# First pair of each part of the down projection by seven products, a reordered plain pair ahead of it, and operand forms fetched in place

## The chip, the cores and the metric

The kernel runs on one core of one Trainium2 chip. The metric is device time in microseconds (us) of one execution; lower is better. TensorE is called PE below, VectorE DVE, ScalarE ACT, GpSimd POOL and SyncE SP, as the profile's page calls them.

## The reference: what is computed

One decoder layer over 512 prompt tokens and 8 sample tokens (520 columns in all, `NTOK`), width 2048, feed-forward width 5632, all in fp32. The part that matters here is the end of the layer:

```python
xn2 = rmsnorm(h, norm_ffn)
gu = xn2 @ w_gate_up
h = h + (jax.nn.silu(gu[..., :D_FF]) * gu[..., D_FF:]) @ w_down
y = rmsnorm(h, norm_final)
```

The last product, `@ w_down`, is the down projection. It follows the gate and up projections and ends just ahead of the final norm and the stores.

## The kernel before

**Precision.** Every fp32 operand is cut into a high part, which ACT rounds (`act.copy` to fp32r), and a low part, which DVE subtracts. A product of 128 by 128 weights with 260 columns (`HALF`) takes three matmuls for each 128 rows of the inner dimension: high by high, high by low, low by high. These are lines 1225 to 1227, in `passes`.

**Tiling.** Work goes by pairs of output tiles of 128 rows (`Pair`), with the inner dimension halved and the columns halved: a 2 by 2 by 2 block product, A11 to A22 for weights and B11 to B22 for activations. Activations in the two cut parts are called forms (`forms[name]` is a high and a low tile). A plain pair takes eight block products. A pair in Strassen's scheme (Winograd's variant) takes seven, M1 to M7, with weights S1 to S4 (sums of A blocks, `add`, line 1247) and forms T1 to T4 (differences of B blocks, computed once). `FORM` names what each product multiplies; `STEADY` gives the order M1, M4, M7, M6, M5, M2, M3.

**Parts.** The down projection splits its inner dimension into three parts (`SIZES` = 7, 7 and 8 steps of 128 for each half), since not all forms fit into SBUF. Each part goes through all eight pairs of output tiles, in the order `ORDER`, and adds to the residual in `mix` (line 1818 adds one operand, line 1819 the second). Forms of a part come from `a_d` in DRAM, where POOL wrote them during the gate and up projections (`to_dram`, lines 1410 to 1413, after `gated`, line 1404).

**A change of parts, before.** `cross` takes two plain pairs: the last of the old part and the first of the new one. Forms are replaced one by one, as soon as the old part has read them for the last time. The scheme between is `run`, over the six pairs left (seven in the last part). `fetch` (line 1776) brings a form from `a_d` into staging tiles `st` (spare rows of `mix` in the first part), two steps to a DMA of POOL's queue; `fill` lets ACT cast the staging into the high tile (line 1785) and DVE write the low one (line 1786). The tables `TAIL`, `LAST` and `HEAD` say after which product of a pair which loads (`+`), cuts, sums and fills are issued.

**Order and buffers.** From the out projection on, instructions stand on each engine in the order of the code. In `strassen`, step i issues the sum of weights for product i + 4, the cut of weights for product i + 3 (ACT line 1218, DVE line 1219), the product i, and then what combines it (`combine`, lines 1270 to 1275, and `out`). Cut weights go round four pairs of buffers (three of `wpl`, one of an extra pool), so a cut waits until PE has read the buffer four cuts back. Products accumulate in eight PSUM banks, five of them called `dn` and taken in turn. Weights come through SP's queue, one block of A to a DMA, into three `raw` buffers and one for A21.

Of the kernel before, what the change touches and what calls it, by code (L numbers as in the profile page):

```python
# [69 lines left out]
def decoder_kernel(ctx, tc, x_prompt, x_sample, state_delta, state_conv, state_pool, norm_mix, w_in,  # L70
# [1158 lines left out]
    class Pair:  # L1229
# [51 lines left out]
        def plain(self, hook):  # L1281

            w = self.w
            a, (b0, *c) = [pst()[:, :HALF] for _ in range(2)], [pst()[:, :HALF] for _ in range(3)]
            passes(a[0], w["A11"], "B11")
            passes(a[1], w["A21"], "B11")
            hook(0)
            for i in range(2):
                act.copy(cm[:, i, :], a[i])
            passes(b0, w["A12"], "B21")  # L1290
            passes(c[0], w["A11"], "T1", stop=False)
            self.cut("A22")
            hook(1)
            self.out(0, 0, cm[:, 0, :], b0)
            passes(c[1], w["A21"], "T1", stop=False)
            hook(2)
            passes(c[0], w["A12"], "B22", start=False)
            b1 = pst()[:, :HALF]
            passes(b1, w["A22"], "B21")
            hook(3)  # L1300
            self.out(0, 1, cm[:, 0, :], c[0])
            self.out(1, 0, cm[:, 1, :], b1)
            passes(c[1], w["A22"], "B22", start=False)
            hook(4)
            self.out(1, 1, cm[:, 1, :], c[1])
# [51 lines left out]
    def strassen(pairs, r21, hook, extra, order=FIRST):  # L1357
# [8 lines left out]
        for i, (q, n) in enumerate(steps):  # L1366
            j = i % 7
            hook(q, j)
            if q + 1 < len(pairs):
                swap = q + 2 == len(pairs) and order is FIRST  # L1370
                name = {0: "A21", 2: "A11", 3: "A12" if swap else "A22", 4: "A22" if swap else "A12"}.get(j)
                if name:
                    pairs[q + 1].load(name, r21 if name == "A21" else None)
            (p, name), (p4, name4) = block(i + 3), block(i + 4)
            pool_ = extra if i % 4 == 0 else wpl
# [3 lines left out]
            if name and (name != "S4" or lastly):  # L1379
                p.cut(name, pool_)  # L1380
# [4 lines left out]
            if name == "S4" and not lastly:  # L1385
                p.cut(name, pool_)
# [186 lines left out]
    strassen(ops, r21o, between, sc0, STEADY)  # L1573
# [187 lines left out]
    stage, spare, staged = [], [], {}  # L1761

    def fetch(name, part_):

        n = SIZES[part_]
        staged[name] = []
        for r in range(0, n, 2):
            k = min(2, n - r)
            if part_ == 0:
                st = rows[len(spare) % len(rows)]  # L1770
                spare.append(name)
            else:
                st = stage[-1][1].tile([P, NTOK], F32, tag="st", name="st", bufs=7)
            st = st.rearrange("p (k c) -> p k c", k=2)[:, 0:k, :]
            fp = sum(SIZES[:part_]) + r
# [238 lines left out]
```

## Time and profile before

| what | value |
|---|---|
| time, median of 3 runs | 2176.09 us (2175.66 to 2178.06) |
| profiled execution | 2173.9 us, span 2172.2 us |
| PE busy | 2139.6 us (99%), 17801 matmuls |
| DVE busy | 1733.3 us (80%) |
| ACT busy | 953.1 us (44%) |
| POOL busy | 450.1 us (21%) |
| mean granted TensorE clock | 0.999 |

The span runs from the first to the last instruction of the profiled execution; its time has 1.7 us around the span. PE's share says where the bound is: there is hardly a moment without a matmul. The down projection begins with the first change of parts at about 1673 us and ends at about 2150 us.

### The profile page before, as it was taken

The page shows a single profiled execution, that of the slowest core. Times are in us where ns is not written, and L with a number is a line of the kernel's source. Part 1 is how long each engine was busy: PE and PEld are TensorE (multiplying, and loading weights), DVE is VectorE, ACT ScalarE, POOL GpSimd, SP SyncE. Part 2 cuts the span into 40 slices and gives each one's busy share as a digit, 9 for nine tenths or more (in the row PEclk, how much of TensorE's full clock was granted, in tenths as well). Part 3 has the DMA queues.
Part 4 walks back from the last instruction along what each step waited for, and adds up shares of the span by engine and source line. Part 5 has one row for each costly group of instructions (what it writes and reads, how often), then busy time and mean ns, then how long its engine had stood idle before and what let it go on. Part 6 is the DMA issues. An engine that isn't in the chain of part 4 may idle for free.

```text
span 2172.2 us, 42935 instructions
## 1 busy us (share of the span) xinstructions
PE 2139.6 (99%) x17801; PEld 2131.8 (98%) x17801; DVE 1733.3 (80%) x2513; ACT 953.1 (44%) x1493; POOL 450.1 (21%) x515
## 2 busy tenths in 40 slices
PE   7999999999999999999999999999999999999998
PEld 6999999999999999999999999999999999999998
DVE  7675657656499978988888888888877798887997
ACT  6434553433265444433434434434334444435444
POOL 2201110101022211333233233232013302003110
PEclk9999999999999999999999999999999999999999
DMA  8343233323445443545545555454446736438333
GB/s 262 95 119 84 81 94 104 92 68 92 132 118 159 150 129 98 156 139 154 156 142 158 149 151 156 142 157 137 130 143 184 245 107 207 114 103 242 95 107 118
DMA packets 443808, 297.03 MB, mean 137 GB/s; under 512 B 26540, under 2 KB 424773, under 8 KB 440269
## 3 DMA queue, kind: packets, MB, share of 16 engines
q1 hardware_dynamic: 424653, 220.87, 35.9%
q0 software_dynamic: 17968, 72.77, 10.3%
q8 instruction: 139, 2.28, 0.4%
q10 hardware_dynamic: 992, 0.66, 0.1%
q14 instruction: 56, 0.46, 0.1%
HBM read 251.47 MB, written 43.43 MB: 136 GB/s over the span
## 4 chain that ended last, share of the span: by engine, by line
PE 85%; DVE 8%; ACT 2%; DMA 2%; issue 1%; POOL 0%; DVEq 0%; ACTq 0%; POOLq 0%
PE dn L1225 19%; PE dn L1226 19%; PE dn L1227 19%; PE mm L179 7%; PE mm L180 7%; PE mm L181 7%; DVE lo L1219 3%; PE dn L853 1%; ACT hi L1218 1%; DVE raw L1247 1%; DMA raw<-in_w_down_dram 1%; DMA st<-a_d 1%; DVE mixb L1818 0%; PE dn L963 0%; DVE mixb L214 0%
## 5 line engine op out<-in xcount | busy, mean ns | idle before, releaser
L1218 ACT CAST hi<-raw 128x1024 fp32r<-128x1024 f32 (+1 forms) x422 | 427.3, 1027 | 402.0 <-DVE raw L1247 200.1
L1219 DVE TENSOR_TENSOR lo<-raw,hi 128x1024 fp32r<-128x1024 f32 (+1 forms) x422 | 530.0, 1277 | 89.3 <-ACT hi L1218 87.9
L179 PE MATMUL mm<-xh,hi 128*128 128x256 f32 (+1 forms) x1280 | 379.2, 296 | 0.9 <-ACT xh L456 0.9
L180 PE MATMUL mm<-xl,hi 128*128 128x256 f32 (+1 forms) x1280 | 362.0, 283 | 1.6 <-DVE xl L359 1.3
L181 PE MATMUL mm<-xh,lo 128*128 128x256 f32 (+1 forms) x1280 | 361.9, 283 | 0.0
L180 PEld LDWEIGHTS mm<-xl,hi 128*128 128x128 f32 x1280 | 242.1, 189 | 2.9 <-DVE xl L359 2.2
L179 PEld LDWEIGHTS mm<-xh,hi 128*128 128x128 f32 x1280 | 241.7, 189 | 1.7 <-ACT xh L456 1.1
L181 PEld LDWEIGHTS mm<-xh,lo 128*128 128x128 f32 x1280 | 241.0, 188 | 0.0
L1227 PE MATMUL dn<-b21h,lo 128*128 128x260 f32 x620 | 175.6, 283 | 0.0
L1247 DVE TENSOR_TENSOR raw<-raw 128x1024 f32<-128x1024 f32 (+1 forms) x130 | 173.8, 1337 | 2.2
L1225 PE MATMUL dn<-b21h,hi 128*128 128x260 f32 x620 | 175.4, 283 | 0.0
L1226 PE MATMUL dn<-b21l,hi 128*128 128x260 f32 x620 | 175.0, 282 | 0.4 <-DVE b21l L1786 0.4
L1227 PE MATMUL dn<-b11h,lo 128*128 128x260 f32 x612 | 173.2, 283 | 0.0
L1225 PE MATMUL dn<-b11h,hi 128*128 128x260 f32 x612 | 173.1, 283 | 0.0
L1226 PE MATMUL dn<-b11l,hi 128*128 128x260 f32 x612 | 172.6, 282 | 0.0
L148 DVE TENSOR_TENSOR lo<-raw,hi 128x1024 fp32r<-128x1024 f32 (+2 forms) x86 | 101.6, 1185 | 85.5 <-ACT hi L146 85.0
L1225 PE MATMUL dn<-T1h,hi 128*128 128x260 f32 x556 | 157.9, 284 | 0.0
L1226 PE MATMUL dn<-T1l,hi 128*128 128x260 f32 x556 | 157.6, 284 | 0.0
L1227 PE MATMUL dn<-T1h,lo 128*128 128x260 f32 x556 | 156.7, 282 | 0.0
L1225 PE MATMUL dn<-B22h,hi 128*128 128x260 f32 x548 | 155.2, 283 | 0.0
L1226 PE MATMUL dn<-B22l,hi 128*128 128x260 f32 x548 | 155.0, 283 | 0.0
L1227 PE MATMUL dn<-B22h,lo 128*128 128x260 f32 x548 | 154.1, 281 | 0.4 <-DVE lo L1219 0.4
(643 smaller groups left out, 6438.8 us busy)
## 6 DMA issues: line engine op xcount, KB each, us to landing
raw<-in_w_gate_up_dram SPq DMA_DIRECT2D x134, 512.0 KB, 3.8
raw<-in_w_in_dram SPq DMA_DIRECT2D x80, 512.0 KB, 3.9
a_d<-mixa POOLq DMA_DIRECT2D x22, 1040.0 KB, 5.4
mixb<-in_w_gate_up_dram SPq DMA_DIRECT2D x42, 512.0 KB
raw<-in_w_down_dram SPq DMA_DIRECT2D x48, 448.0 KB, 4.1
raw<-in_w_out_dram SPq DMA_DIRECT2D x25, 512.0 KB, 3.9
st<-a_d POOLq DMA_DIRECT2D x49, 260.0 KB, 6.9
raw<-in_w_down_dram SPq DMA_DIRECT2D x24, 512.0 KB, 4.4
```

The lines of the kernel that those rows point to most:

```text
L148: dve.tensor_tensor(lo[:, r], raw[:, r], hi[:, r].bitcast(F32), op=ALU.subtract)
L179: te.matmul(acc[ci], wh, hi[k][:, c0:c1], start=(k == 0), stop=False)
L180: te.matmul(acc[ci], wh, lo[k][:, c0:c1], start=False, stop=False)
L181: te.matmul(acc[ci], wl, hi[k][:, c0:c1], start=False, stop=(k == len(w) - 1))
L853: te.matmul(yp[:, ck(c)], xt_[:, ck(c)], cur[:, ck(c)], start=True, stop=True)
L1218: act.copy(hi, raw)
L1219: dve.tensor_tensor(lo, raw, hi.bitcast(F32), op=ALU.subtract)
L1225: te.matmul(acc, wh[:, k, :], xf[:, k, :], start=start and k == 0, stop=False)
L1226: te.matmul(acc, wh[:, k, :], xg[:, k, :], start=False, stop=False)
L1227: te.matmul(acc, wl[:, k, :], xf[:, k, :], start=False, stop=stop and k == wh.shape[1] - 1)
L1247: dve.tensor_tensor(r[name], r[a], r[b], op=op)
```

## The change

The first pair of each part is taken by seven products, as the pairs behind it are. So only the last pair of the old part is plain, and `cross` holds that one alone: eight products instead of sixteen. Three pairs (of 7, 7 and 8 steps) each lose one block product.

The plain pair is put into another order: both products with B11 come first, then both with T1 (the form takes the place of B12 there), then both with B21, then both with B22, and hooks stand ahead of each product. Its first three accumulators come from the other PSUM pool (`ps_mm`).

Forms are fetched in place: one DMA for a whole form goes straight into the low tile, ACT casts from there into the high tile, and DVE writes the difference back over the low tile. There is no staging. The DMA therefore waits until PE has read the low tile for the last time. The fills of the last two forms, B21 and B22, come in two halves during the first pair of the new part (`HEAD`).

The extra pool of the weight buffers is opened once and stays, and every fourth cut goes there, counted over the whole down projection (`fourth`). The residual's rows are loaded pair by pair. In the last part the running sum of squares starts with the other tile of the first pair, and POOL adds squares for seven pairs of eight rather than six of seven.

The rows below are instructions as they stand on one engine. First DVE in the middle change of parts, before: from the cut of A12 of the new part's plain pair (`lo`, 128x896) on. `b21l` and `B22l` are low tiles of forms, L1818 and L1819 add results into the residual, L1247 is a sum of weights.

```order
L1219 TENSOR_TENSOR lo<-raw,hi 128x896
L1786 TENSOR_TENSOR b21l<-st,b21h 128x520 x3
L1786 TENSOR_TENSOR b21l<-st,b21h 128x260
L1818 TENSOR_TENSOR mixa<-mixa,cm 128x260
L1819 TENSOR_TENSOR mixa<-mixa,dn 128x260
L1786 TENSOR_TENSOR B22l<-st,B22h 128x520 x3
L1786 TENSOR_TENSOR B22l<-st,B22h 128x260
L1219 TENSOR_TENSOR lo<-raw,hi 128x896
L1818 TENSOR_TENSOR mixa<-mixa,cm 128x260
L1819 TENSOR_TENSOR mixa<-mixa,dn 128x260
L1219 TENSOR_TENSOR lo<-raw,hi 128x896
L1247 TENSOR_TENSOR sg<-raw,sg 128x896
```

The same two forms after the change, again on DVE in the middle change of parts. L1821 and L1822 are the former L1818 and L1819, L1789 the former L1786. The first row is the cut of S2; the cut of S4 follows right behind the last row.

```order
L1219 TENSOR_TENSOR lo<-raw,hi 128x896
L1789 TENSOR_TENSOR b21l<-b21l,b21h 128x520 x2
L1219 TENSOR_TENSOR lo<-raw,hi 128x896
L1789 TENSOR_TENSOR b21l<-b21l,b21h 128x520
L1789 TENSOR_TENSOR b21l<-b21l,b21h 128x260
L1219 TENSOR_TENSOR lo<-raw,hi 128x896
L1247 TENSOR_TENSOR raw<-raw 128x896
L1789 TENSOR_TENSOR B22l<-B22l,B22h 128x520 x2
L1270 TENSOR_TENSOR cm<-cm,dn 128x260
L1271 TENSOR_TENSOR cm<-cm,dn 128x260
L1821 TENSOR_TENSOR mixa<-mixa,cm 128x260
L1822 TENSOR_TENSOR mixa<-mixa,dn 128x260
```

The two fills moved from the plain pairs into a pair of seven products, between the cuts of S2, S1 and A12, the sum of S4 and the four adds that combine M6. The cut of S4 stands behind all of these.

Second, POOL's queue in the middle change of parts, before: the fetches of two forms, each in four DMAs into staging (`mixa` loads of the residual stand far ahead).

```order
L1776 DMA st<-a_d 128x2x260 x3
L1776 DMA st<-a_d 128x260
L1776 DMA st<-a_d 128x2x260 x3
L1776 DMA st<-a_d 128x260
L1776 DMA st<-a_d 128x2x260 x3
L1776 DMA st<-a_d 128x260
L1776 DMA st<-a_d 128x2x260 x3
L1776 DMA st<-a_d 128x260
```

The same queue after the change, all seven forms:

```order
L1780 DMA T4l<-a_d 128x7x260
L1780 DMA T3l<-a_d 128x7x260
L1780 DMA T2l<-a_d 128x7x260
L1780 DMA b11l<-a_d 128x7x260
L1780 DMA T1l<-a_d 128x7x260
L1780 DMA b21l<-a_d 128x7x260
L1780 DMA B22l<-a_d 128x7x260
```

Four DMAs of a form became one, and the target is the form's low tile.

Third, DVE in the first change of parts, before: the end of the gate and up projections' last pair (L1394) and `gated` (L1404), which releases three tensor instructions of POOL in `to_dram`.

```order
L1786 TENSOR_TENSOR b21l<-mixb,b21h 128x260
L1394 TENSOR_TENSOR mixa<-cm,dn 128x260
L1404 TENSOR_TENSOR mixa<-mixa,sg 128x1040
L1786 TENSOR_TENSOR B22l<-mixb,B22h 128x520 x3
L1786 TENSOR_TENSOR B22l<-mixb,B22h 128x260
L1219 TENSOR_TENSOR lo<-raw,hi 128x896
```

And after, where L1409 and L1419 are the former L1394 and L1404:

```order
L1409 TENSOR_TENSOR mixa<-cm,dn 128x260
L1419 TENSOR_TENSOR mixa<-mixa,sg 128x1040
L1247 TENSOR_TENSOR raw<-raw 128x896
L1219 TENSOR_TENSOR lo<-raw,hi 128x896
L1789 TENSOR_TENSOR b21l<-b21l,b21h 128x520 x2
L1219 TENSOR_TENSOR lo<-raw,hi 128x896
```

What follows `gated` is now the start of the new part's pair of seven products, with the sum and the cut that it needs (S1, S2).

The core of the diff:

```diff
         def plain(self, hook):
             w = self.w
-            a, (b0, *c) = [pst()[:, :HALF] for _ in range(2)], [pst()[:, :HALF] for _ in range(3)]
+            a, c0 = [ps_mm.tile([P, HALF], F32, tag="mm", name="mm") for _ in range(2)], ps_mm.tile(
+                [P, HALF], F32, tag="mm", name="mm")
+            m = cm[:, 0, :], cm[:, 2, :]
+            hook(0)
             passes(a[0], w["A11"], "B11")
+            hook(1)
             passes(a[1], w["A21"], "B11")
...
+            act.copy(m[0], a[0])
             hook(2)
-            passes(c[0], w["A12"], "B22", start=False)
...
+            passes(c0, w["A11"], "T1", stop=False)
+            act.copy(m[1], a[1])
             hook(3)
...
+            c1 = pst()[:, :HALF]
+            passes(c1, w["A21"], "T1", stop=False)
             hook(4)
-            self.out(1, 1, cm[:, 1, :], c[1])
+            b = [pst()[:, :HALF] for _ in range(2)]
+            passes(b[0], w["A12"], "B21")
+            hook(5)
+            passes(b[1], w["A22"], "B21")
+            self.out(0, 0, m[0], b[0])
+            hook(6)
+            passes(c0, w["A12"], "B22", start=False)
+            self.out(1, 0, m[1], b[1])
+            hook(7)
+            passes(c1, w["A22"], "B22", start=False)
+            self.out(0, 1, m[0], c0)
+            hook(8)
+            self.out(1, 1, m[1], c1)
...
     def fetch(name, part_):
-        n = SIZES[part_]
-        staged[name] = []
-        for r in range(0, n, 2):
...
-            pool.dma_start(st, a_d[fp:fp + k, :, QUARTER.index(name), :].rearrange("k p c -> p k c"))
-            staged[name].append((r, st))
+        n, fp = SIZES[part_], sum(SIZES[:part_])
+        pool.dma_start(forms[name][1][:, 0:n, :].bitcast(F32),
+                       a_d[fp:fp + n, :, QUARTER.index(name), :].rearrange("k p c -> p k c"))
+
+    def fill(name, part_, k0=0, k1=8):
         hi, lo = forms[name]
-        for r, st in staged.pop(name):
-            k = st.shape[1]
-            act.copy(hi[:, r:r + k, :], st)
-            dve.tensor_tensor(lo[:, r:r + k, :], st, hi[:, r:r + k, :].bitcast(F32), op=ALU.subtract)
+        for k in range(k0, min(k1, SIZES[part_]), 2):
+            r = slice(k, min(k + 2, SIZES[part_]))
+            act.copy(hi[:, r, :], lo[:, r, :].bitcast(F32))
+            dve.tensor_tensor(lo[:, r, :], lo[:, r, :].bitcast(F32), hi[:, r, :].bitcast(F32), op=ALU.subtract)
...
-    TAIL = {0: ("+A21",), 2: ("+A11",), 3: ("+A12",), 4: ("+A22",), 5: ("A11",), 6: ("A21",)}
-    LAST = {0: ("+A11", "+A21", "+A12", "T3"), 1: ("+A22", "B11"), 2: ("A11",), 3: ("T1", "A21"), 4: ("A12", "B21", "<B22")}
-    HEAD = {0: ("B22", "+A11", "+A22", "+A21"), 1: ("+A12",), 2: ("A11", "S3", "T2"), 3: ("A22",), 4: ("-S3", "S2")}
+    TAIL = {0: ("+A21",), 2: ("+A11", "<T4"), 3: ("+A12", "<T3"), 4: ("+A22", "<T2"), 5: ("A11",), 6: ("A21", "T4")}
+    LAST = {0: ("n+A11", "n+A21", "T3"), 1: ("A12",), 2: ("n+A22", "A22", "<B11", "T2"), 3: ("n+A12", "nS3", "nA11"),
+            4: ("<T1", "nA22"), 5: ("B11",), 6: ("<B21",), 7: ("n-S3", "nS2", "T1"), 8: ("<B22",)}
+    HEAD = {1: ("B21:0",), 2: ("B21:4",), 3: ("B22:0",), 4: ("B22:4",)}
...
-        last.cut("A12")
-        fill("T4", part_)
-        last.plain(lambda step: turn(LAST[step], dps[part_][0], r21, part_))
-        if done:
-            done()
-        dps[part_][0].plain(lambda step: turn(HEAD[step], dps[part_][1], r21_, part_))
+        last.plain(lambda step: turn(LAST.get(step, ()), part_, last, dps[part_][0], r21))
...
-    cross(0, gu[-1], lambda: gated(FP - 1), lambda: to_dram(FP - 1))
+    cross(0, gu[-1])
+    gated(FP - 1)
+    to_dram(FP - 1)
...
     for part_ in range(1, len(SIZES)):
-        run(dps[part_ - 1][1:-1], r21s[1], None, STEADY, dps[part_ - 1][-1])
+        run(dps[part_ - 1][:-1], lambda q: r21s[1], heading(part_ - 1), STEADY, dps[part_ - 1][-1], part_)
         cross(part_, dps[part_ - 1][-1])
...
-    run(dps[-1][1:], r21s[1], sums, LASTLY)
+    run(dps[-1], lambda q: r21s[1], heading(len(SIZES) - 1, sums), LASTLY)
```

In the tables after the change, `<` is a fetch, a bare form name its fill, `n` marks the new part's first pair, `+` a load, `-` or A a cut, S a sum, and `B21:4` the fill of the second half.

More of the change, by code (lines that the diff above doesn't have):

```diff
@@ L1385, in strassen @@
             if name == "S4" and not lastly:
-                p.cut(name, pool_)
+                p.cut(name, where())
     def gate_out(i, half, a, b):
@@ L1849, in turn @@
             elif x[0] in "A-":
-                p.cut(x.strip("-"))
+                p.cut(x.strip("-"), where())
             elif x[0] == "S":
@@ L1854, in turn, with run @@
                 fetch(x[1:], part_)
+            elif x[-2] == ":":
+                k = int(x[-1])
+                fill(x[:-2], part_, k, k + 4)
             else:
                 fill(x, part_)
-    def run(pairs, r21, hook=None, order=FIRST, last=None):
-        if stage:
-            stage.pop()[0].close()
+    def run(pairs, r21, hook=None, order=FIRST, last=None, part_=0):
         def during(q, j):
```

83 lines of the change are left out of this document (34 added, 49 removed).

## The prediction

> **What bounds the kernel now.** I read the page's busy times first, then who PE waited for, then busy times of three stretches of the down projection; after that the timelines of DVE, ACT and POOL for prices, and the view of the staging tile for fetches.
>
> ```profile
> PE 2139.6 (99%) x17801; PEld 2131.8 (98%) x17801; DVE 1733.3 (80%) x2513; ACT 953.1 (44%) x1493; POOL 450.1 (21%) x515
> PE dn L1227 <- DVE lo L1219: 4.0, 4, 2.0
> PE dn L1226 <- DVE b21l L1786: 0.4, 1, 0.4
> L1226 PE MATMUL dn<-b21l,hi 128*128 128x260 f32 x620 | 175.0, 282 | 0.4 <-DVE b21l L1786 0.4
> core 0: us, PE busy (x) PEld busy (x) DVE busy (x) ACT busy (x) POOL busy (x), PEclk, DMA share, GB/s
> 1800.00:1960.00 160.00, 160.00 (x1334) 160.00 (x1333) 136.82 (x202) 69.38 (x95) 18.88 (x28) 1.00 0.50 141
> 1960.00:2020.00 60.00, 59.59 (x495) 59.30 (x494) 45.58 (x71) 31.06 (x48) 19.88 (x28) 1.00 0.72 218
> 2020.00:2118.00 98.00, 97.82 (x814) 97.61 (x813) 92.75 (x108) 49.82 (x61) 17.92 (x10) 1.00 0.39 106
> ```
>
> PE bounds the kernel. From 1800 to 1960 us, the second part and the change of parts before it, it never idles: 1334 matmuls in 160 us are 0.120 us each at full clock. In the last change of parts (1960 to 2020) it idles 0.4 us, the whole of its wait for `b21l`. DVE is the next engine: 95% busy in the last part. So a matmul taken away is worth its 0.120 us as long as DVE, ACT and the DMAs still have their pieces ready in time. That is what has to be counted.
>
> **What the change removes.** Three block products: 3 matmuls by 7, 7 and 8 steps, together 66 matmuls. 66 x 0.120 = 7.9 us. A product takes 21 x 0.120 = 2.52 us with 7 steps and 24 x 0.120 = 2.88 us with 8. The wait for `b21l` also goes, since PE now wants that form eight products after its fetch may start:
>
> ```profile
> 1995.37 0.39 PE L1226 MATMUL dn<-b21l,hi 128*128 128x260 f32 x1 [0.41 <-DVE b21l L1786]
> ```
>
> That is 0.4 us, and 0.1 for the refill behind it: the first matmul after the wait takes 0.39 us, where the mean of its group is 0.28. Removed in all: 8.4 us.
>
> **What it adds to DVE.** A plain pair costs DVE four cuts and eight adds of 260 columns; a pair by seven products costs seven cuts, four sums and eleven adds. Prices are distances between starts, since instructions overlap. The first stretch is inside the second part (7 steps), the next the last change of parts (8 steps):
>
> ```profile
> 1779.65 0.42 DVE L1270 TENSOR_TENSOR cm<-cm,dn 128x260 f32<-128x260 f32 x1 [1.62 <-PE dn L1227]
> ...
> 1781.37 2.08 DVE L1219 TENSOR_TENSOR lo<-raw,hi 128x896 fp32r<-128x896 f32 x2
> 1783.38 0.42 DVE L1818 TENSOR_TENSOR mixb<-mixb,cm 128x260 f32<-128x260 f32 x1
> 1783.90 0.42 DVE L1819 TENSOR_TENSOR mixb<-mixb,dn 128x260 f32<-128x260 f32 x1
> 1784.24 0.42 DVE L1275 TENSOR_TENSOR cm<-cm,dn 128x260 f32<-128x260 f32 x1
> 1784.58 1.08 DVE L1247 TENSOR_TENSOR sg<-raw,sg 128x896 f32<-128x896 f32 x1
> 1785.58 1.08 DVE L1219 TENSOR_TENSOR lo<-raw,hi 128x896 fp32r<-128x896 f32 x1
> ...
> 1987.10 1.22 DVE L1219 TENSOR_TENSOR lo<-raw,hi 128x1024 fp32r<-128x1024 f32 x1
> 1988.24 2.52 DVE L1786 TENSOR_TENSOR T1l<-st,T1h 128x520 fp32r<-128x520 f32 x4
> 1990.68 1.21 DVE L1219 TENSOR_TENSOR lo<-sg,hi 128x1024 fp32r<-128x1024 f32 x1
> ...
> 1690.46 2.25 DVE L1786 TENSOR_TENSOR T1l<-mixb,T1h 128x520 fp32r<-128x520 f32 x4
> 1692.63 1.08 DVE L1219 TENSOR_TENSOR lo<-mixb,hi 128x896 fp32r<-128x896 f32 x1
> ...
> 1966.30 0.94 ACT L1218 CAST hi<-sg 128x896 fp32r<-128x896 f32 x1 [3.67 <-PE dn L1226]
> 1985.56 1.05 ACT L1218 CAST hi<-raw 128x1024 fp32r<-128x1024 f32 x1
> ```
>
> With 7 steps: M6's four adds 1.72 (1779.65 to 1781.37), a cut or sum 1.00, an `out` of two adds 0.86, M5's three adds 1.20, a fill 2.17. With 8 steps: a cut 1.14, a fill 2.44. Half a fill of two instructions is 1.20 or 1.22; the odd rest of 7 steps, 0.95. A high cast takes 0.94 or 1.05 on ACT. So DVE needs 11 x 1.00 + 1.72 + 1.20 + 2 x 0.86 = 15.6 us for a pair for which PE takes 7 x 2.52 = 17.6. The first pair of a part has B21 and B22 to fill on top, 4.3 us: 19.9 against 17.6. It can't keep pace; what counts is its lead.
>
> **The middle change, as a running sum.** Let PE start the plain pair at 0; products end at 2.52, 5.04 and so on. The cut of S3 needs the buffer of A12, which PE frees when its seventh product ends, at 17.64. Up to there DVE has waits to catch up in. Then everything stands in a row: ACT's cast 0.95; cut S3 1.00, sum S2 1.00, fill T1 2.17, two `out` 1.72; sum S1, cut S2 2.00; half of B21 1.20; cut S1 1.00; the rest of B21 0.95; cut A12, sum S4 2.00; half of B22 1.20; M6's adds 1.72; cut S4 1.00. That comes to 17.9, so S4 is ready at 35.55. PE wants it for the seventh product of the new pair, at 20.16 + 6 x 2.52 = 35.28. Late by 0.27.
>
> What follows makes it a bit later: rest of B22, cut A11, M5's adds, sum S3, cut A22 are 5.15 in two products of 5.04, and then twice 2.86 in 2.52. Together 0.79, and after that DVE gains again. This change of parts costs 1.06 us of PE.
>
> **The last change** has 8 steps behind it, so cuts cost more but products give more room. The same row sums to 19.71: 17.64 + 19.71 = 37.35 against 20.16 + 6 x 2.88 = 37.44. Just in time; afterwards 0.08 + 2 x 0.26 less the 0.09 left, 0.51 us.
>
> **The first change** has a plain pair of 8 steps with single adds (0.34 to 0.42), so S3's buffer is free at 20.16 and the new pair starts at 23.04. But `gated` now stands in the row, and what it releases on POOL now meets it:
>
> ```profile
> 1700.86 1.24 DVE L1404 TENSOR_TENSOR mixa<-mixa,sg 128x1040 f32<-128x1040 f32 x1
> 1702.02 4.47 DVE L1786 TENSOR_TENSOR B22l<-mixb,B22h 128x520 fp32r<-128x520 f32 x4
> 1702.19 1.69 POOL L1410 TENSOR_TENSOR mixa<-mixa 128x520 f32<-128x520 f32 x1 [0.28 <-DVE mixa L1404]
> 1703.95 1.09 POOL L1411 TENSOR_TENSOR mixa<-mixa 128x260 f32<-128x260 f32 x1
> 1705.12 1.08 POOL L1412 TENSOR_TENSOR mixa<-mixa 128x260 f32<-128x260 f32 x1
> ```
>
> `gated` takes 1.16 until the next start. The fill beside POOL's three instructions takes 4.47 instead of 2.17: 2.3 us. The row is 17.9 - 1.72 + 0.8 + 1.16 + 2.3 = 20.4, so S4 comes at 20.16 + 20.4 = 40.6, wanted at 23.04 + 15.12 = 38.16. Late by 2.4, and 0.79 behind it: 3.2 us. Before, two plain pairs covered the same 2.3 us. The Trainium skill's page "SBUF — State Buffer", section "SBUF: two separate sides", says that POOL and a DVE instruction with two SBUF inputs exclude each other for whole instructions. By that rule DVE would lose POOL's 3.9 us rather than 2.3, and the change would cost 1.6 us more. The trace has the smaller number, and I take it.
>
> Waits of this kind come in about eleven pieces, each with the 0.1 us of refill: 1.1. Sum of what is given back: 1.06 + 0.51 + 3.2 + 1.1 = 5.9 us.
>
> **Fetches in place.** The DMA waits on POOL's queue until PE has read the form. Behind it there wait only later fetches, in the first part `to_dram` and the residual's loads, none needed within ten products. B11's fetch may start at 5.04. Its fill, two `out`, cut S3, sum S2, fill T1 and two `out` (9.8 us) must end by 25.2, when M7 takes the PSUM bank that the last `out` frees. So there are 10.4 us for issue and landing. What they take in the last change of parts:
>
> ```profile
> L1776 POOL DMA_DIRECT2D st<-a_d x28: 704/712/727, 1964.0 to 1998.8; - x28
> DMA to landing us min/median/max: 4.7/7.0/8.1
> 1966.09 4.24 POOL L1776 DMA_DIRECT2D st<-a_d  x6 [1.39 <-issue]
> 1974.65 0.63 ACT L1785 CAST T4h<-st 128x520 fp32r<-128x520 f32 x1 [0.99 <-DMA st<-a_d]
> ```
>
> A DMA of a quarter lands after 4.7 to 8.1 us. The last three quarters of T4 were issued from 1966.09 and the last landed by 1974.65: 8.6 us. I take 8.6 for a whole form: hidden, with 1.8 us to spare. Bounds are 4.7 and, with three more quarters at 1 us each behind the slowest, 11. The Trainium skill's page "DMA: Bandwidth & Descriptors", section "Anatomy of one DMA — SWDGE (gpsimd) path", would give 2.0 us plus 932 KB at 436 GB/s, an estimate of 4.1 us, and a quarter 2.6. Measured quarters take 4.7 and more, so the measurement decides.
>
> Edits at nothing: ACT's three more cuts for each pair (44% busy); weights (the raw buffers come free as late as now, seven products ahead); POOL's sums of squares, which move one pair later. Were that last cover gone, a sum beside a cut would cost some 0.5 us.
>
> **Sum.** -8.4 + 5.9 = -2.5 us. The profiled execution's 2173.9 us (span and 1.7) becomes 2171.4. The runs' median, 2176.1, stands 2.2 above it, and the same difference gives 2173.6.
>
> **Rivals.** *DVE keeps up.* POOL's instructions fall where DVE waits anyway, and the row is a few tenths shorter for each product. Then PE keeps 7.9 to 8.4 us: 2167.7 to 2168.2. For it: the late points miss by 0.3 and by nothing in two changes of three. Against it: the first pair needs more of DVE than PE takes. I give 0.32 to the cases in which at most 4 us are given back.
>
> *Fetches land late.* The place is B11 and T1 in the two later changes, where the cover ends at 10.4 us. The price is 1 us of PE for each us more, in each of the two. At 14 us, beyond what the quarters show, it is 2 x 3.6 = 7.2 more: 2180.8, slower. The gain is gone from 10.4 + 2.5 / 2 = 11.7 us on. For it: weights and forms share the DMA engines, busy 72% from 1960 to 2020, and a fetch can no longer run ahead into staging. Against it: the 8.6. The same page of the Trainium skill on SBUF warns, in "SBUF: two separate sides", that POOL writes a DMA's descriptors through the ports that DVE can lock; no row here separates this. Chance 0.18 for a loss above 4.4 us by this or a mishap beside it.
>
> *It does not do what it says.* Excluded: 66 matmuls fewer stand on PE in the changed program.
>
> **How the numbers follow.** A measurement of this kernel tells about 0.2% (4.4 us) from no change. My forecast of 2173.6 lies within; its own range, 2.9 to 8 us given back, is 2170.6 to 2175.7. Faster by more needs less than 4 us given back: 0.32. Slower by more needs the late landing: 0.18. Within: 0.50. The range goes down to 2168.5 (nearly nothing given back) and up to 2180.
>
> **What would show it.** PE with about 17735 matmuls; in the new part's first pair waits for `lo` of S4 of about 2.4, 0.3 and 0 us, then small ones for A22, S3 and S2; one-DMA fetches landing in 8 to 9 us. I am wrong on DVE if PE never waits there, wrong on the fetches if ACT's casts of `b11h` or `T1h` wait for DMAs and PE waits in the plain pair or on M7, and wrong on POOL if the first change costs no more than the middle one.

## Result, and the profile after

The change made the kernel slower. Its median is 2186.51 us (five runs, 2183.82 to 2187.58) against 2177.68 us for the kernel before in the same session (five runs, 2175.66 to 2179.94): a ratio of 1.0044, with a 95% interval of 1.0034 to 1.0055. The forecast was 2173.6 us, in a range that ended at 2180.0.

The first lines of the page of the kernel after, its span and the busy time and number of instructions of each engine:

```profile
span 2185.6 us, 42685 instructions
PE 2140.7 (98%) x17735; PEld 2129.5 (97%) x17735; DVE 1753.4 (80%) x2543; ACT 958.5 (44%) x1499; POOL 414.0 (19%) x452
```

The 66 matmuls are gone (17801 less 17735), and DVE works 20 us more. What PE waited for in the first change of parts (1690 to 1740 us), as total, times and longest:

```profile
PE dn L1225 <- ACT hi L1218: 5.9, 2, 4.4
PE dn L1227 <- DVE lo L1219: 3.1, 4, 1.7
```

The same view for the second and third change together (1845 to 2050 us):

```profile
PE dn L1227 <- DVE lo L1219: 5.2, 5, 1.4
```

In the second and third change these are the waits of the first pair of seven products for S2 and S4 (0.53 and 1.39 us, then 0.98 and 1.13) and, in the third, one of the second pair for S2 (1.14). Waits for DVE's low parts were forecast. The 5.9 us for ACT's high parts were not. To see the whole loss I took the distances between the starts of matmuls and, for all that are over 0.15 us, added up what each is over 0.12 us. This counts waits, refills and a slower clock together, and I call it the *excess*. It is 13.9 us in the first change, 3.2 in the second and 4.4 in the third, 21.5 in all; before it was 0, 0 and 1.3. So 21.5 - 1.3 - 7.9 for the matmuls gone is 12.3 us, where the span grew by 13.4. The medians differ by 8.8 only; the profiled execution of before, 2173.9 us, lies below its median. Below, totals come from medians and places from profiles.

PE in the first change, its rows with a wait of over a microsecond:

```profile
1715.35 0.39 PE L1227 MATMUL dn<-B22h,lo 128*128 128x260 f32 x1 [1.70 <-DVE lo L1219]
1719.41 0.39 PE L1225 MATMUL dn<-b11h,hi 128*128 128x260 f32 x1 [1.51 <-ACT hi L1218]
1728.86 0.58 PE L1225 MATMUL dn<-T4h,hi 128*128 128x260 f32 x1 [4.43 <-ACT hi L1218]
```

The first is S4 in the first pair of seven products. The other two stand behind that pair: they are the first two products of the *second* pair (A11 and A22), for which the forecast counted DVE's work but not when the weights land. ACT's two casts ahead of them say why:

```profile
1718.42 0.94 ACT L1218 CAST hi<-raw 128x896 fp32r<-128x896 f32 x1 [5.18 <-DMA raw<-in_w_down_dram]
1727.87 0.94 ACT L1218 CAST hi<-raw 128x896 fp32r<-128x896 f32 x1 [8.51 <-DMA raw<-in_w_down_dram]
```

ACT waits for the second pair's weights, in the end for 8.5 us. The chain that ended last has one DMA of 16.39 us at this place, the load of A22:

```profile
1711.38 16.39 DMA raw<-in_w_down_dram
```

POOL's timeline shows what it issues meanwhile, behind the store of `to_dram` (first row): `heading`'s 14 loads of the residual.

```profile
1707.02 0.58 POOL L1428 DMA_DIRECT2D a_d<-mixa  x1 [0.30 <-POOL mixa L1427]
1707.60 1.10 POOL L1967 DMA_DIRECT2D mixa<-h_d  x2
1708.69 2.65 POOL L1967 DMA_DIRECT2D mixb<-h_d  x5
...
1721.32 0.54 POOL L1967 DMA_DIRECT2D mixa<-h_d  x1 [0.29 <-DMA mixb<-h_d]
```

In the code two rows are loaded for each pair, but POOL waits for nothing of PE or DVE there, so all 14 go out as fast as POOL issues them. Before, they went out in a row too, but later. The first of them had waited 5.79 us for DVE's fill of `T2l`, whose staging lay in rows that these loads write:

```profile
1712.86 0.56 POOL L1958 DMA_DIRECT2D mixa<-h_d  x1 [5.79 <-DVE T2l L1786]
```

Without staging that wait is gone. Now they begin at 1707.60, right beside the three weights of the second pair that SP asks for from 1708.31 on. The DMA issues of 1707 to 1732 us, with count, size and the median from issue to landing (of those loads whose landing the profile knows):

```profile
mixb<-h_d POOLq DMA_DIRECT2D x8, 260.0 KB, 10.1
mixa<-h_d POOLq DMA_DIRECT2D x6, 260.0 KB, 6.3
raw<-in_w_down_dram SPq DMA_DIRECT2D x3, 448.0 KB, 10.0
```

Of the three weights one landing is known, that of the first, after 10.0 us; the second is the 16.39 us of the chain. The page's part on DMA issues, over the whole kernel after, has a median of 4.1 for such loads:

```profile
raw<-in_w_down_dram SPq DMA_DIRECT2D x48, 448.0 KB, 4.1
```

So these two weights took more than twice their usual time. Three stretches of the first change (busy time and count of each engine, the granted clock, DMA share, GB/s) show what it did to PE:

```profile
1700.00:1719.00 19.00, 15.79 (x127) 15.15 (x126) 16.08 (x21) 7.46 (x13) 10.64 (x15) 1.00 0.77 252
1719.00:1734.00 15.00, 9.21 (x42) 8.49 (x43) 8.14 (x13) 3.35 (x5) 2.10 (x4) 0.66 0.54 180
1734.00:1750.00 16.00, 16.00 (x135) 16.00 (x135) 15.13 (x22) 6.90 (x8) 0.00 (x0) 1.00 0.43 115
```

42 matmuls in 15 us, where before there were 128. The granted clock of 0.66 is a mean. Behind each of the two waits for ACT it was 0.50, and matmuls start 0.22 us apart for some 3 us:

```profile
1720.50:1723.50 3.00, 2.96 (x13) 2.96 (x14) 2.09 (x4) 0.00 (x0) 1.07 (x2) 0.50 1.13 332
1730.00:1733.80 3.80, 3.80 (x17) 3.80 (x18) 3.59 (x7) 1.22 (x2) 0.00 (x0) 0.50 0.00 0
```

The six waits of the first change add up to 9.0 us; the other 4.9 of the excess are these slow matmuls and refills.

### The profile page after: what moved, and what is told of

Same layout as the page of the kernel before. It is cut to its first block, busy times and chain, and to the rows that moved or that the text cites. A ratio compares the mean times of both kernels' runs of the same rounds, so it can differ in the third digit from the quotient of the medians.

```text
span 2185.6 us, 42685 instructions
## 1 busy us (share of the span) xinstructions
PE 2140.7 (98%) x17735; PEld 2129.5 (97%) x17735; DVE 1753.4 (80%) x2543; ACT 958.5 (44%) x1499; POOL 414.0 (19%) x452
## 3 DMA queue, kind: packets, MB, share of 16 engines
q0 software_dynamic: 16960, 72.76, 10.4%
## 4 chain that ended last, share of the span: by engine, by line
PE 87%; DVE 7%; ACT 2%; issue 2%; DMA 1%; POOL 0%; SPq 0%; ACTq 0%; DVEq 0%; POOLq 0%
PE dn L1225 20%; PE dn L1227 20%; PE dn L1226 20%; PE mm L179 7%; PE mm L180 7%; PE mm L181 7%; DVE lo L1219 3%; PE dn L853 1%; DMA raw<-in_w_down_dram 1%; DVE raw L1247 1%; ACT hi L1218 1%; PE mm L1225 0%; PE mm L1226 0%; PE mm L1227 0%; DVE b21l L1789 0%
## 5 line engine op out<-in xcount | busy, mean ns | idle before, releaser
L1218 ACT CAST hi<-raw 128x1024 fp32r<-128x1024 f32 (+1 forms) x431 | 436.4, 1026 | 443.7 <-DVE raw L1247 224.2
L1219 DVE TENSOR_TENSOR lo<-raw,hi 128x1024 fp32r<-128x1024 f32 (+1 forms) x431 | 540.7, 1276 | 91.2 <-ACT hi L1218 89.4
L1247 DVE TENSOR_TENSOR raw<-raw 128x1024 f32<-128x1024 f32 (+1 forms) x136 | 180.8, 1329 | 2.3
L1225 PE MATMUL dn<-b11h,hi 128*128 128x260 f32 x546 | 155.2, 284 | 1.5 <-ACT hi L1218 1.5
L1227 PE MATMUL dn<-b11h,lo 128*128 128x260 f32 x546 | 155.3, 285 | 0.6 <-DVE lo L1219 0.6
L1226 PE MATMUL dn<-b11l,hi 128*128 128x260 f32 x546 | 154.6, 283 | 0.0
L1406 ACT ACTIVATE sg<-sg 128x260 f32<-128x260 f32 x88 | 37.0, 422 | 257.2 <-DVE sg L1405 257.2
L146 ACT CAST hi<-raw 128x1024 fp32r<-128x1024 f32 (+1 forms) x85 | 87.4, 1028 | 142.1 <-PE mm L180 131.8
L1425 POOL TENSOR_TENSOR mixa<-mixa 128x520 f32<-128x520 f32 x22 | 51.2, 2329 | 504.4 <-DVE mixa L1419 504.4
L1227 PE MATMUL dn<-B22h,lo 128*128 128x260 f32 x504 | 142.1, 282 | 4.7 <-DVE lo L1219 4.7
L1225 PE MATMUL dn<-T1h,hi 128*128 128x260 f32 x512 | 145.5, 284 | 0.0
L1226 PE MATMUL dn<-T1l,hi 128*128 128x260 f32 x512 | 145.2, 284 | 0.0
```

Source lines behind the costliest of these rows:

```text
L146: act.copy(hi[:, r], raw[:, r])
L1218: act.copy(hi, raw)
L1219: dve.tensor_tensor(lo, raw, hi.bitcast(F32), op=ALU.subtract)
L1225: te.matmul(acc, wh[:, k, :], xf[:, k, :], start=start and k == 0, stop=False)
L1226: te.matmul(acc, wh[:, k, :], xg[:, k, :], start=False, stop=False)
L1227: te.matmul(acc, wl[:, k, :], xf[:, k, :], start=False, stop=stop and k == wh.shape[1] - 1)
```

## The experiments

Two things had to be explained, the 13.9 us of the first change and the 7.6 of the two others. My theory for the first: the residual's loads, all at once, hold up the second pair's weights. For the others: the form fetches slow the weights, so that DVE's row starts late. The rivals were that DVE's longer row alone does it, or POOL's work beside it. Each ratio below is to the kernel before in the same session, whose median was 2175.91 us for the first four runs, 2176.41 for e5_paced_col to e8_raw and 2176.64 for e9_s3_early to e12_pad_before.

**Pacing the residual's loads** (e1_paced).

```
+    tok = const.tile([P, 1], F32, name="tok")
...
-            if part_ == 0 and j == 1:
+            if part_ == 0 and j == 4:
+                pool.tensor_copy(tok, cm[:, 1, 0:1])
                 for m in (2 * ORDER[q + 1], 2 * ORDER[q + 1] + 1):
```

> The changed kernel, but POOL loads the residual's rows pair by pair: ahead of each two loads it copies one column that M6's adds of the running pair have written, so it can't run ahead. Theory A (the 14 loads in a row fill the DMA engines and hold up the weights of the second pair in the first change of parts): PE's two waits for the high part (1.5 and 4.4 us) and the phases at 0.66 of the clock behind them go, a loss of 13.9 us in the first change becomes about 3.5, and the time falls by 10 us to about 2176. Rival B (DVE is late with its sums and so releases the raw buffers late; the loads are harmless): A22 still lands some 10 us after its buffer comes free, and the time falls by less than 3 us.

Measured: 2180.74 us, ratio 1.0024 (1.0014 to 1.0034). The first change's excess fell from 13.9 to 3.5 us. PE's waits from 1690 to 1750 us, all of them:

```profile
PE dn L1228 <- DVE lo L1220: 2.1, 2, 1.7
```

None is for ACT any more. The middle one of the three stretches:

```profile
1719.00:1734.00 15.00, 13.28 (x105) 12.82 (x106) 14.56 (x22) 5.82 (x7) 0.51 (x1) 1.00 0.43 125
```

The granted clock stays at 1.00. But the time is still 4.8 us above the kernel before of its session, where the change had 8.8 (5.8 us lie between the two medians of different sessions). Much of the rest was lost outside the down projection: in the gate and up projections matmuls stood 0.1208 us apart instead of 0.1202. The runs e5_paced_col and e6_shift look for that.

**Loading eight of the residual's rows earlier** (e2_early), during the gate and up projections.

```
         if q % 2 == 1 and j in (0, 3) and q < 32:
             next(states[q // 2])
+        if j == 2 and 30 <= q < 40:
+            m = (4, 5, 10, 11, 12, 13, 14, 15)[q - 30] if q < 38 else None
+            if m is not None:
+                pool.dma_start(mix[m], h_d[m])
...
-            if part_ == 0 and j == 1:
+            if part_ == 0 and j == 1 and ORDER[q + 1] in (4, 0, 1):
```

> The changed kernel, but eight of the fourteen late residual rows are loaded during the gate and up projections (one for each pair), where their tiles lie idle; six remain behind the first change. Theory A: the burst shrinks from 3.6 to 1.6 MB, so most of the 10 us comes back: 2176 to 2179. Rival B: no change beyond 3 us.

Measured: 2176.32 us, ratio 1.0001 (0.9992 to 1.0011); the excess is 4.3, 2.8 and 3.9 us. Two quite different ways to take the burst away leave the first change at 3.5 to 4.3 us. The burst cost about 10 us by the excess (13.9 to 4.3). By the time it is 8.4 us if each median is set against before in its own session (8.8 and 0.4 above it).

**DVE without the low parts of B21 and B22** (e3_nolow, on top of e1_paced).

```
-            dve.tensor_tensor(lo[:, r, :], lo[:, r, :].bitcast(F32), hi[:, r, :].bitcast(F32), op=ALU.subtract)
+            if name not in ("B21", "B22"):
+                dve.tensor_tensor(lo[:, r, :], lo[:, r, :].bitcast(F32), hi[:, r, :].bitcast(F32), op=ALU.subtract)
```

> Paced loads as in the run with paced loads, and DVE leaves out the low part of the forms B21 and B22 (8 instructions a change of parts, some 4.3 us); their low tiles keep what was fetched. Theory A (what is left of PE's waits is DVE's row of work, which the prediction summed): the waits for S4 in all three changes (1.7, 1.4 and 1.1 us) go, those for S2 and the small ones behind them too, and the time lies 6 to 8 us below paced loads alone: about 2169. Rival C (the waits left come from weights that land late): at most 2 us less than paced loads alone.

Measured: 2173.95 us (2171.5 to 2181.3), ratio 0.9997 (0.9986 to 1.0007), 6.8 us less than e1_paced. The excess falls from 3.5, 2.8 and 4.6 to 2.5, 0.2 and 0.9 us. So DVE's row is what PE waits for in the later changes. In the first one the wait for S4 is gone too; 1.8 of the 2.5 us left stand at the second pair's A22.

**Each fetch brings one step only** (e4_thin, on top of e1_paced). DVE and ACT work as before; only the DMAs have less to do.

```
     def fetch(name, part_):
         n, fp = SIZES[part_], sum(SIZES[:part_])
+        n = 1
```

> Paced loads as in the run with paced loads, and each fetch brings one of a form's 7 or 8 steps only (the other steps keep old numbers); all casts and subtractions stay. Theory C (three fetches of about 1 MB in a row slow the weights from 4.3 to 8.5 us, DVE gets to the cut of S3 2.7 us late in the last change, and its row then ends late): weights land in about 4.3 us, the waits in the second and third change go down from 3.2 and 4.4 to about 1 us each, and the time is 4 to 6 us below paced loads alone. Theory A' (DVE's row alone, however the weights land): less than 1.5 us below.

Measured: 2176.77 us, ratio 1.0004 (0.9994 to 1.0013), 4.0 us less than e1_paced. The excess in the later changes falls from 2.8 and 4.6 to 1.4 and 1.7. DMA issues of 1955 to 2020 us, of the kernel after:

```profile
raw<-in_w_down_dram SPq DMA_DIRECT2D x5, 448.0 KB, 8.5
T2l<-a_d POOLq DMA_DIRECT2D x1, 1040.0 KB, 10.9
```

And of e4_thin:

```profile
raw<-in_w_down_dram SPq DMA_DIRECT2D x3, 448.0 KB, 3.8
T2l<-a_d POOLq DMA_DIRECT2D x1, 130.0 KB, 3.6
```

One landing is known in each row of weights, and it is that of the same load, A11 of the old part's last pair: 8.5 us beside whole fetches and 3.8 beside thin ones. The load that DVE's row hangs on is the new pair's A22 (512 KB). SP issued it at 1990.34 us in the kernel after and at 1980.44 in e4_thin; ACT cast it 6.7 and 4.3 us later:

```profile
1997.07 1.05 ACT L1218 CAST hi<-raw 128x1024 fp32r<-128x1024 f32 x1 [4.71 <-DMA raw<-in_w_down_dram]
1984.73 1.06 ACT L1219 CAST hi<-raw 128x1024 fp32r<-128x1024 f32 x1 [1.87 <-DMA raw<-in_w_down_dram]
```

Both theories are right, then: DVE's row sets the end, and late transfers set its start. Thin fetches also bring B11 itself sooner; e8_raw below takes the weights alone. DVE in the third change of the kernel after:

```profile
1998.15 1.22 DVE L1219 TENSOR_TENSOR lo<-raw,hi 128x1024 fp32r<-128x1024 f32 x1 [2.13 <-ACT hi L1218]
1999.30 2.52 DVE L1789 TENSOR_TENSOR b11l<-b11l,b11h 128x520 fp32r<-128x520 f32 x4
...
2003.48 1.22 DVE L1219 TENSOR_TENSOR lo<-sg,hi 128x1024 fp32r<-128x1024 f32 x1
...
2022.18 1.30 DVE L1789 TENSOR_TENSOR B22l<-B22l,B22h 128x520 fp32r<-128x520 f32 x2
```

The first row is the cut of the new pair's A22, the third that of S3, with which my running sum began. From S3's start to the end of S4's cut (2022.18) it took 18.7 us; the sum, 19.71 less ACT's cast of 1.05, says the same. But it began at 2003.48. The plain pair's seventh product ended at 1999.7, so that the sum had it begin at 2000.8. DVE idled for A22 until 1998.15 (ACT's cast had waited 4.7 us for its DMA) and did in a row with S3 what I had put into its waits. In the second change S3's cut began at 1855.67, 2.0 us late in the same way.

The row explains 2.6 of the 4.4 us in the third change. Another 1.4 stand in the second pair, at M6, and have another cause. POOL's sum of squares and the two instructions of DVE beside it, the sum S1 and the cut of S2, then PE:

```profile
2032.87 1.54 POOL L1808 TENSOR_TENSOR sq<-sq,sq 128x520 f32<-128x520 f32 x1 [29.39 <-ACT sq L1800]
2032.02 1.22 DVE L1247 TENSOR_TENSOR raw<-raw 128x1024 f32<-128x1024 f32 x1
2033.16 2.34 DVE L1219 TENSOR_TENSOR lo<-raw,hi 128x1024 fp32r<-128x1024 f32 x1
2035.55 0.39 PE L1227 MATMUL dn<-T2h,lo 128*128 128x260 f32 x1 [1.14 <-DVE lo L1219]
```

The cut took 2.34 us instead of 1.22, though ACT's cast for it had ended at 2031.25. The same wait stands in e4_thin (1.13 us). In the kernel before it was 0.18 us. In e3_nolow DVE's row is earlier: POOL's sum then meets an `out`, whose first add takes 1.54 us instead of 0.42, the cut takes 1.22, and PE does not wait there.

**Pacing without a new tile, and the new tile alone** (e5_paced_col, shown against e1_paced; e6_shift, made from the kernel before).

```
-                pool.tensor_copy(tok, cm[:, 1, 0:1])
+                pool.tensor_copy(prm[:, 156:157], cm[:, 1, 0:1])
```

```
     epst = const.tile([P, 1], F32, name="epst")
+    tok = const.tile([P, 1], F32, name="tok")
...
     pool.memset(epst, EPS)
+    pool.memset(tok, 0.0)
```

> As e1_paced, POOL loads the residual's rows pair by pair behind a copy of one column of `cm`, but the copy goes into a column of `prm` that nothing else uses, so no tile is added and no later tile moves. e1_paced lost the burst (first change 13.9 to 3.5 us of matmul waits) but gained only 5.8 us of 10, since its matmuls everywhere stood 0.1208 instead of 0.1202 us apart. Theory (the four bytes of the added tile shift every later tile, and that costs about 5 us): 2175 to 2177 us, matmuls 0.1202 us apart. Rival (pacing the loads itself costs the 5 us): 2180 to 2181, as e1_paced.

> The kernel before the change with one tile of four bytes a partition added, set once and used by nothing. Theory (where the later tiles begin sets the distance of matmuls): about 17750 matmuls by 0.0005 us and more, 4 to 7 us: 2179.5 to 2183, with matmuls 0.1205 to 0.1208 us apart in the gate and up projections. Rival (the added tile is free, e1_paced lost its 5 us in another way): 2175 to 2177, no difference.

Measured: e5_paced_col 2175.72 us (ratio 1.0000, 0.9991 to 1.0009), e6_shift 2180.17 (1.0018, 1.0009 to 1.0027). One tile that nothing uses (its four bytes move the tiles behind it by 32) costs the kernel before 3.8 us, and pacing without it gives 9.5 us (8.8 above before has become 0.7 below). It is a matter of matmuls at large. The busy times from 1000 to 1660 us, of the kernel before:

```profile
1000.00:1660.00 660.00, 660.00 (x5490) 660.00 (x5489) 566.26 (x607) 266.19 (x326) 178.83 (x138) 1.00 0.49 145
```

And of e6_shift:

```profile
1000.00:1660.00 660.00, 660.00 (x5464) 660.00 (x5463) 564.44 (x607) 264.74 (x325) 173.09 (x136) 1.00 0.50 145
```

In the same 660 us PE starts 26 matmuls fewer. The kernel after has x5490 there, as before, so this is no part of what the change costs. It does mean that e3_nolow and e4_thin, which have the tile, are to be compared with e1_paced alone.

**POOL's work out of the first pair** (e7d_defer): eight rows early as in e2_early, the other six paced as in e5_paced_col, and `to_dram(FP - 1)` put off to the second pair.

```
     gated(FP - 1)
-    to_dram(FP - 1)
...
+                if q == 1:
+                    to_dram(FP - 1)
+                if ORDER[q + 1] in (4, 0, 1):
```

> The change, with eight rows of the residual loaded during the gate and up projections, the other six pair by pair, and POOL's work on the last piece of g (`to_dram`) put off from the first pair of seven products to the second. Theory (in the first change DVE's row is lengthened by 2.3 us beside POOL's three instructions): the fill of `B22l`/`b21l` beside them falls from 4.5 to 2.2 us, the matmuls' waits in the first change fall from 4.2 us (e2_early) to 1.5 to 2.2, the time to 2173 to 2174.5. Rival (the row is late in any case, the fill's length is absorbed by DVE's waits): as e2_early, 2176.

Measured: 2172.92 us, ratio 0.9986 (0.9977 to 0.9995). The first change's excess falls to 1.2 us, from 4.3 in e2_early and 3.4 in e5_paced_col. DVE's instructions beside POOL's work, in the timeline of the kernel after:

```profile
1702.73 2.21 DVE L1219 TENSOR_TENSOR lo<-raw,hi 128x896 fp32r<-128x896 f32 x1
1704.87 2.42 DVE L1789 TENSOR_TENSOR b21l<-b21l,b21h 128x520 fp32r<-128x520 f32 x2
```

The same two in e7d_defer:

```profile
1703.13 1.08 DVE L1219 TENSOR_TENSOR lo<-raw,hi 128x896 fp32r<-128x896 f32 x1
1704.13 1.30 DVE L1789 TENSOR_TENSOR b21l<-b21l,b21h 128x520 fp32r<-128x520 f32 x2
```

POOL's three instructions cost DVE 1.13 + 1.12 = 2.25 us, and PE 2.2 to 3.1 with what follows.

**A22's weights asked for earlier** (e8_raw, on top of e7d_defer, with one raw buffer more).

```
-    LAST = {0: ("n+A11", "n+A21", "T3"), 1: ("A12",), 2: ("n+A22", "A22", "<B11", "T2"), 3: ("n+A12", "nS3", "nA11"),
+    LAST = {0: ("n+A11", "n+A21", "n+A22", "T3"), 1: ("A12",), 2: ("A22", "<B11", "T2"), 3: ("n+A12", "nS3", "nA11"),
...
+                p.load(x[1:], r21 if x == "+A21" else rawx[0] if x == "+A22" and p is next_ else None)
```

> As e7d_defer, with a fifth raw buffer for the new pair's A22 in the changes of parts, so that its weights are asked for with A11's and A21's, two products earlier, ahead of B11's fetch. Theory (in the later changes DVE's row starts 2.7 us late because A22's weights land late beside the fetches): the waits in the second and third change fall from about 7 us together to 2 to 4, the time by 3 to 5 us against e7d_defer: 2168.5 to 2171. Rival (DVE's own row sets the end, or weights land late whenever they are asked for): no difference from e7d_defer, 2173 to 2174.5.

Measured: 2173.66 us (2169.9 to 2180.2), ratio 0.9991 (0.9982 to 1.0000): no gain. The third change's excess fell from 3.7 to 2.0 us, the second's did not (3.2, now 3.7). In the third change ACT cast A22 11.0 us after the plain pair began instead of 14.3, S3's cut began at 19.0 instead of 20.7, and PE's waits for S2 and S4 of the first pair are gone; what is left is mostly the wait beside POOL's sum. This is the late weights' share alone. In the second change SP began to issue the load 4.6 us after the plain pair began instead of 7.4, and ACT cast its weights at 15.1 us instead of 14.6. The DMA engines are full there. Two stretches of the kernel after, the 10 us ahead of the plain pair and its first 17.5 us:

```profile
1825.06:1835.06 10.00, 10.00 (x85) 10.00 (x84) 6.72 (x13) 3.94 (x6) 1.86 (x2) 1.00 0.99 321
1835.06:1852.56 17.50, 17.50 (x149) 17.50 (x148) 14.15 (x22) 10.51 (x20) 2.79 (x3) 1.00 0.95 268
```

In e8_raw the same two stretches have a DMA share of 1.01. With the DMAs this busy, the earlier request waited longer. The view puts ACT's wait for this cast down to PE, which frees the cut buffer; but e4_thin cast A22 at 10.3 us, so the buffer was free by then, and the transfer is the likelier cause. The rival ("weights land late whenever they are asked for") holds in one change of the two.

**S3's cut into DVE's idle time** (e9_s3_early, on top of e7d_defer, with one cut buffer more).

```
-            4: ("<T1", "nA22"), 5: ("B11",), 6: ("<B21",), 7: ("n-S3", "nS2", "T1"), 8: ("<B22",)}
+            4: ("<T1", "n-S3", "nA22", "nS2"), 5: ("B11",), 6: ("<B21",), 7: ("T1",), 8: ("<B22",)}
...
-                p.cut(x.strip("-"), where())
+                p.cut(x.strip("-"), fifth[0] if x == "-S3" else where())
```

> As e7d_defer, with a fifth cut buffer in the changes of parts, used for S3 alone, and the cut of S3 moved from behind the seventh product of the plain pair to the fifth, ahead of the cut of A22, whose weights land late. Theory (from A22's cut on DVE works without a pause up to S4, and each us that leaves this row is a us less of PE's waits; the 3.2 us that DVE idles ahead of A22's cut can take S3's cut): the row is 1.0 us shorter in each change, and each change has up to three late points behind one another that shrink by about that once: the waits fall from 1.2, 3.2 and 3.7 us to about 0.5, 2.0 and 2.5, the time by 2.5 to 4 us to 2169 to 2170.5. Rival (what paces the row is the DMAs' and not DVE's work: T1's or B21's form lands later than the row asks for it): no difference from e7d_defer, 2173.

Measured: 2171.37 us, ratio 0.9977 (0.9968 to 0.9986): quicker than both kernels, and 1.6 us quicker than e7d_defer where 2.5 to 4 was expected. The two runs are of different sessions and their ratios' intervals overlap, so the 1.6 us are not clear of noise. The excess is 0, 2.5 and 5.0 us. What failed is the third change: there A22's weights were cast 16.5 us after the plain pair's start, in e7d_defer after 14.3. PE also waited 0.39 us for the fill of `b11l` behind that cut. This took the gain back.

**Where tiles begin** (e11_pad_best, on top of e9_s3_early; e12_pad_before, made from the kernel before).

```
+    padp = ctx.enter_context(tc.tile_pool(name="padp", bufs=1, side="right"))
+    padt = padp.tile([P, 8], F32, name="padt")
     mpl = ctx.enter_context(tc.tile_pool(name="mpl", bufs=1, side="right"))
...
+    pool.memset(padt, 0.0)
```

> As e9_s3_early, with a pad of 32 bytes a partition ahead of the tiles on the right side of SBUF, so that b11, b21, T4's low part and one cut buffer of the earlier phases begin at multiples of 64 bytes, as the cut buffers of the left side do. Theory (matmuls go 0.1193 to 0.1198 us apart with some forms and 0.1205 to 0.1208 with others by where operands begin, and multiples of 64 are the good places): 3 to 8 us less than e9_s3_early. Rival (only the left side's cut buffers matter, or something other than multiples of 64): the same within 1.5 us.

> The kernel before the change with the same pad of 32 bytes alone. Theory (multiples of 64 bytes): 2168 to 2173, with matmuls 0.1193 to 0.1198 us apart in the gate and up projections instead of 0.1202. Rival: 2175 to 2177.5, no difference.

Measured: 2176.00 us (0.9999, 0.9991 to 1.0008) and 2180.87 (1.0019, 1.0010 to 1.0027): the pad costs 4.6 and 4.2 us. My theory of multiples of 64 bytes fell. By the addresses in the built programs, the cut buffers of the left side begin at multiples of 64 bytes in the kernel before and `b11`, `b21` on the right side 32 bytes off; matmuls stand 0.1202 us apart in the gate and up projections. The added tile moved the left side 32 bytes off too; the pad moved the right side onto multiples of 64. Both made the two sides alike, and both gave 0.1208 us there. In the second part of the down projection (1760 to 1960 us) it is not so: PE starts 1669 matmuls in both, and 1666 in the kernel before. So alike sides are not slower everywhere. Which operand it is that must stand apart, and why, stays open.

## Why the prediction was wrong, point by point

**The step that failed** stands under "Edits at nothing": "weights (the raw buffers come free as late as now, seven products ahead)", together with "in the first part `to_dram` and the residual's loads, none needed within ten products". Both say when a transfer is asked for or needed; neither asks what else the DMA engines carry at that moment. The residual's loads are not needed soon, but they held up weights that were (10.0 and 16.4 us to land): about 10 us by the excess, shown by e1_paced, e2_early and e5_paced_col. In the other changes the new pair's A22 landed late beside the fetches (6.7 us from issue to cast in the third, 4.3 with thin fetches). That put the start of DVE's row 2.0 and 2.7 us late: 4.0 us by e4_thin.

**A second term at nothing** was "POOL's sums of squares, which move one pair later", with "some 0.5 us" for a sum beside a cut. One stood beside the cut of S2 in the last part's second pair, lengthened it by 1.1 us and cost PE 1.4.

**What it removes** was right: 66 matmuls at 0.120 us, the wait for `b21l` gone.

**DVE's row** was right in size (18.7 us measured in the third change, 19.71 - 1.05 = 18.7 summed), and e3_nolow shows that PE waits for it. Its start was wrong: "Up to there DVE has waits to catch up in" fails once A22's weights come late. Then A22's cut, B11's fill and two `out`, 4.9 us in the second change, move from the waits into the row. So the forecast of 1.06 and 0.51 us, with refills, became an excess of 3.2 and 4.4. The late start also brought a wait that the forecast did not list, for S2 at the first pair's fourth product (0.53 and 0.98 us). It follows from the row: summed to the end of S2's cut, the row leaves 1.2 and 1.4 us up to that product, less than the 2.0 and 2.7 by which it began late.

**POOL beside DVE** was right in size: 2.3 us forecast, 2.25 measured. The waits of the first pair in the first change, 0.42 for S1, which was not forecast, and 1.70 for S4, are together near the forecast's 2.4 with refills. The Trainium skill's "SBUF — State Buffer", section "SBUF: two separate sides", has a POOL instruction that reads SBUF and a DVE instruction with two SBUF inputs exclude each other for whole instructions. I had held POOL's spans against that rule (here 2.09 + 1.49 + 1.08 = 4.7 us) and taken the trace to contradict it. It does not, since those spans can hold POOL's own waits for DVE. In the same trace an instruction of L1426 (128x260) takes 0.75 us in 14 of its 22 places and 1.5 to 1.8 in the others, and the one of 128x520 takes 1.31 us in e7d_defer (at 1728.25 us). 1.31 + 0.75 + 0.75 = 2.8 us is an estimate of POOL's work without waits, and DVE lost 2.25.

**Fetches in place** as such were near the forecast. Whole forms landed after 5.7 to 10.9 us, where I took 8.6, and the slowest one with a deadline (T1, 9.5 us in the third change) stays below the cover of 10.4. ACT's cast of `T1h` did wait 0.89 us for that DMA, which the forecast had named as a sign, but PE waited for no form. So the rival "fetches land late" did not come about in its own place. Its argument that "weights and forms share the DMA engines" was the right one, but I drew it for the forms and not for the weights. The Trainium skill's "DMA: Bandwidth & Descriptors", section "Anatomy of one DMA — SWDGE (gpsimd) path", gives a fit by which a thin fetch of 130 KB would take about 2.3 us, an estimate. In e4_thin it took 2.3 to 4.9, so the estimate is met by the quickest of them only.

**The sum.** Forecast given back: 5.9 us. Measured excess over before: 20.2 (21.5 - 1.3), of which about 10 is the burst and 2 to 3 POOL's work in the first change. The other 7 or so are DVE's row in all three changes, about 4 of it from late transfers, and POOL's sum in the third, 1.4 where before had 0.4. What the forecast gave for the first change, 3.2 us and refills, is close to what the paced runs left there (3.4 and 3.5).

## What to carry to other kernels

A step that moves transfers is costed by what flies beside it: list every queue's issues in the window, those without a near deadline too, and ask which urgent load they would meet. Loads on an engine that waits for nothing go out as a burst, whatever the order in the code; tie them to the work's pace or send them in a quiet phase earlier. A buffer that is taken away may have been what held such loads back. A running sum needs its start checked as carefully as its terms, and the start hangs on the last operand to land, not on the one that comes to mind.

## What the runs showed of the hardware that was not expected

After a wait of PE of 1.5 us, four microseconds behind one of 1.7 and followed by one of 0.6, and again after one of 4.4 us, the granted clock fell to 0.50, and matmuls stood 0.22 us apart for about 3 us. A wait of 1.7 us alone, in e1_paced, left it at 1.00. The waits themselves were two thirds of the price, 9.0 of 13.9 us.

A tile that nothing uses, and that moves others by 32 bytes, made the kernel 3.8 to 4.6 us slower in three pairs of runs, each of one session (e6_shift and e12_pad_before against before, e11_pad_best against e9_s3_early), and 5.0 in a fourth pair of two sessions (e1_paced against e5_paced_col). In the gate and up projections matmuls stood 0.1208 instead of 0.1202 us apart. An experiment that adds a tile should have a control with the tile alone.
